# The low product of each 64-row score pair on all 128 rows

## The chip, the cores and the metric

The kernel runs on one core of a Trainium2 chip. The metric is the device time of one execution in microseconds (us); the median of the runs is compared. TensorE is called PE below (PEld is its weight load), VectorE DVE, ScalarE ACT, GpSimd POOL and SyncE SP, as the profile does.

## The reference

Two layers of a streaming encoder trunk over 512 tokens of width 2048, all in float32. Each layer normalises its input, multiplies it by one wide weight, and gives the columns to three attention mixers (MLA, DSA and differential attention), whose gated outputs go through an output projection; then a gated embedding is added. Cut to the scores that the change touches:

```python
# MLA: 128 plain features and 64 rotated ones; the rotated key is shared by the 6 heads
q = concat([q[..., :128], rope(q[..., 128:], pos, 64)]);  k = concat([k_nope, rope(k_rope, pos, 64)])
sc = einsum('bqhd,bkhd->bhqk', qb, k) * 192 ** -0.5
# DSA indexer: 8 heads of 64 rows, one key of 64 rows for all
rel = relu(einsum('bqhd,bkd->bqhk', qib, ki));  score = einsum('bqhk,bqh->bqk', rel, wb)
top_val, top_idx = lax.top_k(where(mask, score, NEG_INF), 128)     # the chosen keys of a query
# differential attention: 5 heads of two halves of 64 rows
a1 = softmax(mask(einsum('bqhd,bkhd->bhqk', qb[..., 0, :], k1) * 64 ** -0.5))
a2 = softmax(mask(einsum('bqhd,bkhd->bhqk', qb[..., 1, :], k2) * 64 ** -0.5))
o = einsum('bhqk,bkhd->bqhd', a1 - lam * a2, v)
```

## The kernel before

**Exact products from parts.** PE multiplies float32r values in one pass, which carries only part of float32. So each operand is split into a high part (an ACT copy that rounds) and a low part (what is left, a DVE subtraction), by `split_into`, and `mm3` (lines 369 to 371) forms a product of two split operands in three passes: high by high, high by low, low by high. Nearly all PE work is `mm3`: the input projection (`pp<-g,wh` in the profile), the output projection and the embedding gate, over 16 feature tiles of 128 rows.

**Pairs of 64 rows.** Where the summed dimension has 64 rows, `stack` lays a query's high part in one half of the 128 partitions and its low part in the other (`[hi; lo]` or `[lo; hi]`), and `twice` lays the key's high part in both halves. One pass over 128 rows then gives high by high and low by high. That is the first product of `mm2`, line 376. The second product, line 377, adds high by low: it takes the 64 rows of the query's tile that hold its high part, and the same 64 rows of a tile with the key's low part:

```python
a = TOP if half == 0 else LOW
PE.matmul(ps, q[:, qs], hi[:, :n], start=start, stop=False)      # line 376
PE.matmul(ps, q[a, qs], lo[a, :n], start=False, stop=stop)       # line 377
```

A pair has a width n of 128, 256, 384 or 512 keys, one for each block of 128 queries and the keys it may see. There are 88 pairs in a layer: 6 heads by 4 blocks in MLA, 8 heads by 3 blocks in the indexer (block 0 needs no choice), and 5 heads by 2 halves by 4 blocks in differential attention. So lines 376 and 377 stand in the profile with 176 instructions each.

**Low parts of the keys.** `twice` makes one low part by a DVE subtraction on 64 rows, 512 wide. Called without `lo`, as for the keys that MLA and the indexer share (`keys["r"]`, `keys["i"]`), it lays the low part in both halves, with two subtractions (lines 287 and 289). In differential attention `diff_ready` gives it a tile `kl` for both halves of a head: the low part of the first half goes to the upper 64 partitions, that of the second to the lower 64, one subtraction each (line 287).

**What sets the order.** The projection runs a chunk of weights at a time: SP loads a chunk (`wr`), ACT makes its high part (`wh`), DVE its low part (`wl`, line 363), and PE takes both. Two side streams are recorded between the chunks, each for a share of the projection's time: `mixers()` (MLA, then the indexer, then `heads()`), and `choose()`, which finds the 128 largest scores of each query by 16 rounds of `MAX` and `MATCH_REPLACE` on DVE (lines 786 and 787). `heads()` has the operands of the next head made (`diff_ready`) while the present one ends. A scheduler then orders each engine's instructions by a simulated timeline; on the chip each engine takes its own in that fixed order. All large temporaries are tiles `g` of one pool of 59 slots; scores go to PSUM tiles `at`, projections to `pp`.

Of the kernel before, what the change touches and what calls it, by code (L numbers as in the profile page):

```python
# [33 lines left out]
# columns of w_in  # L34
# [11 lines left out]
def rope_order():  # L46
    """Rows of 64: groups of 8, x1 then x2 of the frequencies 4i, 4i+2, 4i+1, 4i+3."""
    first, freq = [], []
    for r in (0, 2, 1, 3):
        for second in (0, 1):  # L50
            for i in range(8):
                freq.append(4 * i + r)
                first.append(1 - second)
    return np.array(freq), np.array(first)
# [65 lines left out]
class Stream:  # L120
    """Where each chunk [128, kt * cols] of one layer's weight lies in its flat array."""
# [19 lines left out]
def host_arrays(inputs):  # L141
    a = {k: np.asarray(v) for k, v in inputs.items()}

    def chunks(w, cols):
        """[K, n] at columns -> chunk after chunk of [128, 2, n]."""
        k = w.shape[0] // 128
        x = w[:, cols].reshape(k // 2, 2, 128, len(cols))
        return x.transpose(0, 2, 1, 3).reshape(-1)

    w_in = np.stack([np.concatenate([chunks(a["w_in"][i], c) for c in GROUP_COLS]) for i in range(DEPTH)])  # L150

    def square(w):
        return np.stack([np.concatenate([chunks(w[i], np.arange(512 * g, 512 * g + 512)) for g in range(4)])
                         for i in range(DEPTH)])

    order = np.concatenate([128 * m + np.arange(128) for m in MIX_ORDER])
    w_o = square(a["w_o"][:, order])
    w_pg = square(a["w_pg"])
    w_ple = square(a["w_ple"])

    uq, ukv = [], []
    for i in range(DEPTH):
        q, kv = [], []
        for j in range(3):
            h = (2 * j, 2 * j + 1)
            cols = np.concatenate([192 * x + np.arange(128) for x in h] + [192 * x + 128 + PERM_A for x in h])
            x = a["w_uq"][i][:, cols].reshape(3, 128, 384)
            q += [x[:2].transpose(1, 0, 2).reshape(-1), x[2].reshape(-1)]
            cols = np.concatenate([256 * h[0] + np.arange(128)] + [256 * x + 128 + np.arange(128) for x in h])
            kv += [chunks(a["w_ukv"][i], cols), chunks(a["w_ukv"][i], 256 * h[1] + np.arange(128))]  # L170
        uq.append(np.concatenate(q))
        ukv.append(np.concatenate(kv))

    def col(g):
        return g.reshape(-1, 128).T

    cc = np.concatenate([col(a["norm_g"]), col(a["q_norm_g"]), col(a["kv_norm_g"]), col(a["subln_g"]),
                         col(a["final_g"])], axis=1)
    lam = np.stack([a["lam_q1"], a["lam_k1"], a["lam_q2"], a["lam_k2"]], axis=1).reshape(1, DEPTH * 256)
    base = (500000.0 ** (np.arange(32) / 32.0)).astype(np.float32)  # L180
    inv = (np.float32(1.0) / base).astype(np.float32)
    rc = np.zeros((128, 8), np.float32)
    for half in range(2):
        s = slice(64 * half, 64 * half + 64)
        rc[s, 0] = inv[FREQ]
        rc[s, 1] = np.where(FIRST == 1, -1.0, 1.0)
    rc[:32, 2] = 1.0
    for half in range(2):
        rc[64 * half:64 * half + 16, 4] = 1.0
    rc[:, 3] = 1.0 - rc[:, 2]  # L190
    rc[:, 5] = 1.0 - rc[:, 4]
    c = np.ascontiguousarray
    return {
        "x": c(a["x"][0].T), "p": c(a["p"][:, 0].transpose(0, 2, 1)), "positions": c(a["positions"]),
        "w_in": w_in, "w_o": w_o, "w_pg": w_pg, "w_ple": w_ple,
        "w_uq": np.stack(uq), "w_ukv": np.stack(ukv), "cc": c(cc), "lam": c(lam), "rc": rc,
    }
# [3 lines left out]
def trunk(ctx: ExitStack, tc: tile.TileContext, t, out):  # L201
# [66 lines left out]
    def stack(y):  # L268
        """Of the two halves of 64 rows: [hi; lo] of the first, [lo; hi] of the second."""
        res = []  # L270
        for a, b in ((TOP, LOW), (LOW, TOP)):
            o = slot(F32R)
            ACT.activation(o[a], y[a], AF.Copy)
            DVE.tensor_tensor(o[b], y[a], f32(o[a]), op=ALU.subtract)
            res.append(o)
        return res

    def twice(y, half, lo=None):
        """hi of 64 rows in both halves, and lo, there or in both halves as well."""
        a, b = (TOP, LOW) if half == 0 else (LOW, TOP)  # L280
        hi = slot(F32R)
        ACT.activation(hi[a], y[a], AF.Copy)
        ACT.activation(hi[b], y[a], AF.Copy)
        both = lo is None
        if both:
            lo = slot(F32R)
        DVE.tensor_tensor(lo[a], y[a], f32(hi[a]), op=ALU.subtract)
        if both:
            DVE.tensor_tensor(lo[b], y[a], f32(hi[a]), op=ALU.subtract)
        return hi, lo  # L290
# [21 lines left out]
    def col_sums(parts):  # L312
        """sums over the partitions, a column [128 tokens, 1] for each block of the parts"""
# [7 lines left out]
    def rsqrt(dst, src, n, size):  # L321
        """1 / sqrt(mean + eps), from the table's root and a step of Newton's"""
# [12 lines left out]
    def spread(cols):  # L335
        """columns [128 tokens, 4] -> the same row of 512 on every partition, in PSUM."""
# [30 lines left out]
    def mm3(ps, l, r, start, stop):  # L367
        """ps += l^T r to float32's accuracy, of parts that one pass each carries."""
# [4 lines left out]
    def mm2(ps, q, qs, hi, lo, n, half, start, stop):  # L373
        """ps += of 64 rows: q stacked [hi; lo], hi in both halves, lo in this one."""
        a = TOP if half == 0 else LOW
        PE.matmul(ps, q[:, qs], hi[:, :n], start=start, stop=False)
        PE.matmul(ps, q[a, qs], lo[a, :n], start=False, stop=stop)
# [8 lines left out]
    streams, done = [], set()  # L386

    class Side:
        """Work that is emitted between the chunks of a projection, a share of their time."""
# [5 lines left out]
        def step(self):  # L395
            """False where it cannot go on before another chunk."""
# [26 lines left out]
    def products(ps, src, us, load, one):  # L423
        """ps of 16 feature tiles of the source: load(c) gives a chunk's 2 pairs, one(m, k, pair) multiplies."""
        nm = len(ps)
        for c in range(8):
# [6 lines left out]
            else:  # L433
                # A product at a time, so that the first are there early.
# [8 lines left out]
    def group_t(name, layer, stream, first, nm, src, gcol=None):  # L443
        """nm tiles of 128 features by 512 tokens; src: 16 pairs of [128, 512]."""
# [11 lines left out]
    def group_tok(name, layer, stream, first, n, src, gcol):  # L456
        """4 blocks of 128 tokens by n features"""
# [74 lines left out]
    def table(kind, R):  # L532
        """The tables of a branch, times the norm's factor of each token."""
# [8 lines left out]
    def rope(src, cs, rows=slice(0, 128), eng=POOL):  # L542
        """src * cos + swap(src) * sin -> float32 in a temporary."""
# [10 lines left out]
    def soft(ps, n, scale, e):  # L554
        """e = exp(scale * (ps - max)); returns 1 / sum."""
# [7 lines left out]
    def causal(ps, i):  # L563
        """the last 64 keys are hidden from the first 64 queries of block i"""
        DVE.memset(ps[0:64, 128 * i + 64:128 * i + 128], NEG)

    def attend(probs, v):
        """out^T [dv, tokens] in PSUM of probabilities [q, keys] per block; v(kb): pair [128 keys, 128]."""
# [22 lines left out]
    for L in range(DEPTH):  # L591
# [10 lines left out]
        def factors():  # L602
            """the norm's factor of each token, as columns and spread over the partitions"""
# [79 lines left out]
        def mla():  # L683
# [9 lines left out]
            for j in range(3):  # L693
# [30 lines left out]
                for x in range(2):  # L724
# [5 lines left out]
                    for i in range(NB):  # L730
# [4 lines left out]
                        mm2(ps[:, :n], q[2][x], qs, kr[0], kr[1], n, x, False, True)  # L735
# [15 lines left out]
        bias, score = {}, {}  # L751

        def indexer():
# [3 lines left out]
            for x in range(I_H):  # L757
# [4 lines left out]
                for i in range(1, NB):  # L762
# [3 lines left out]
                    mm2(ps[:, :n], q[x % 2], qs, ki[0], ki[1], n, x % 2, True, True)  # L766
# [35 lines left out]
        def diff_ready(x):  # L802
            q = stack(rope(raw.pop(("qc", x)), tab["c"]))
            y = rope(raw.pop(("kc", x)), tab["c"])
            kl = slot(F32R)
            return q, [twice(y, c, kl)[0] for c in range(2)], kl, value_parts("vc", x)

        def diff_probs(x, ops, probs):
            q, k, kl, _ = ops
            for i in range(NB):  # L810
# [5 lines left out]
                for c in range(2):  # L816
                    ps = at()
                    mm2(ps[:, :n], q[c], qs, k[c], kl, n, c, True, True)
# [50 lines left out]
        def heads():  # L869
            """the heads of both mixers; the operands of the next are made ahead"""  # L870
# [147 lines left out]
    def finals(s, R, pool_tiles):  # L1018
        """the tiles times the norm's factors, two at a time"""
# [71 lines left out]
```

## Time and profile before

| what | value |
|---|---|
| median of 3 runs | 2401.24 us (2401.13 to 2401.72) |
| the profiled execution: its span, first to last instruction | 2399.5 us |
| median less that span | 1.7 us |
| mean granted PE clock | 0.993 |
| busy ACT, POOL | 1067.6 us (44%), 486.1 us (20%) |
| DMA, mean over the span | 100 GB/s |

The page gives busy time, not useful time: a PE instruction's duration includes the time that it spends in the pipeline, so PE's rows overlap, and a PE that is shown busy may still start its products further apart than it could. How fast it goes is read from the distance between the starts of neighbouring instructions in the timeline.

### The profile page before, as it was taken

What the parts mean: (1) busy time and instruction counts of PE and PEld (TensorE: products, weight loads), DVE (VectorE), ACT (ScalarE), POOL (GpSimd) and SP (SyncE); (2) the same over time, 40 slices, a digit from 0 to 9 for tenths busy, and PEclk for the clock granted to TensorE, in tenths of its full rate; (3) what the DMA queues carried; (4) which work ended last, traced back from release to release, by engine and by line L of the source; (5) the groups of instructions that cost most, each with busy time, mean ns of one, the idle gap of its engine ahead of it and who ended that gap; (6) DMA issues with size and microseconds to landing.
All of it is one profiled execution on the core that took longest, in us unless ns stands there. A gap on an engine that the chain in (4) does not pass through costs nothing. (4 is left out here: it accounts for less than half of the span.)

```text
span 2399.5 us, 31043 instructions
## 1 busy us (share of the span) xinstructions
PE 2352.9 (98%) x11362; PEld 1956.7 (82%) x11372; DVE 1473.9 (61%) x2846; ACT 1067.6 (44%) x1989; POOL 486.1 (20%) x393
## 2 busy tenths in 40 slices
PE   8999999999999999999999999999999999999997
PEld 6899977777888788878888998777787887888887
DVE  8655557976667734344466555599667676543345
ACT  6444444454555423233345444444545554232444
POOL 4210122111232301011230110211122322220023
PEclk9999999999999999999999999999999999999998
DMA  5233322232233322322322333222222233232234
GB/s 182 73 95 94 121 78 81 84 101 88 97 97 110 112 98 98 105 88 97 97 88 77 92 112 102 81 84 97 82 99 93 97 111 113 97 106 97 97 105 159
DMA packets 88569, 239.03 MB, mean 100 GB/s; under 512 B 9440, under 2 KB 25312, under 8 KB 88416
## 3 DMA queue, kind: packets, MB, share of 16 engines
q1 hardware_dynamic: 84064, 223.41, 28.9%
q0 software_dynamic: 4352, 13.64, 1.5%
q8 instruction: 89, 1.46, 0.3%
q14 instruction: 64, 0.52, 0.1%
HBM read 219.19 MB, written 17.83 MB: 99 GB/s over the span
## 5 line engine op out<-in xcount | busy, mean ns | idle before, releaser
L369 PE MATMUL pp<-g,wh 128*128 128x512 f32 (+1 forms) x2432 | 942.4, 389 | 10.1 <-ACT g L263 6.0
L370 PE MATMUL pp<-g,wh 128*128 128x512 f32 (+1 forms) x2432 | 940.8, 387 | 0.0
L371 PE MATMUL pp<-g,wl 128*128 128x512 f32 (+1 forms) x2432 | 922.4, 388 | 15.3 <-DVE wl L363 15.2
L363 DVE SCALAR_TENSOR_TENSOR wl<-wr,cc,wh 128x512 fp32r<-128x512 f32 (+4 forms) x554 | 437.1, 799 | 327.3 <-ACT wh L362 316.8
L362 ACT ACTIVATE wh<-wr,cc 128x512 fp32r<-128x512 f32 (+4 forms) x554 | 361.8, 661 | 519.1 <-PE pp L370 339.4
L371 PEld LDWEIGHTS pp<-g,wl 128*128 128x128 f32 x2432 | 457.1, 189 | 109.5 <-DVE wl L363 18.5
L369 PEld LDWEIGHTS pp<-g,wh 128*128 128x128 f32 x2432 | 459.2, 189 | 105.7 <-ACT g L263 6.9
L370 PEld LDWEIGHTS pp<-g,wh 128*128 128x128 f32 x2432 | 458.7, 189 | 90.7 <-issue 2.2
L359 DVE TENSOR_TENSOR wl<-wr,wh 128x512 fp32r<-128x512 f32 x288 | 219.1, 771 | 356.1 <-ACT wh L358 332.0
L358 ACT ACTIVATE wh<-wr 128x512 fp32r<-128x512 f32 x288 | 177.9, 629 | 404.7 <-PE pp L370 370.0
L370 PE MATMUL pp<-wl,g 128*128 128x384 f32 (+2 forms) x512 | 158.5, 312 | 0.0
L371 PE MATMUL pp<-wh,g 128*128 128x384 f32 (+2 forms) x512 | 156.9, 310 | 0.0
L546 POOL TENSOR_TENSOR t<-z,cos 128x512 f32<-128x512 f32 (+1 forms) x50 | 71.4, 1429 | 393.6 <-DVE e L822 239.2
L369 PE MATMUL pp<-wh,g 128*128 128x384 f32 (+2 forms) x512 | 147.2, 319 | 0.0
L307 POOL TENSOR_TENSOR acc<-acc,t 128x512 f32<-128x512 f32 x41 | 59.1, 1441 | 298.6 <-ACT t L306 294.9
L264 DVE TENSOR_TENSOR g<-t,g 128x512 fp32r<-128x512 f32 x78 | 104.0, 1337 | 20.8 <-ACT g L263 20.8
L647 POOL DMA_DIRECT2D o_d<-t x32 | 18.2, 570 | 398.5 <-ACT t L645 398.5
L370 PEld LDWEIGHTS pp<-wl,g 128*128 128x128 f32 x512 | 96.6, 189 | 1.2 <-issue 0.4
L369 PEld LDWEIGHTS pp<-wh,g 128*128 128x128 f32 x512 | 93.0, 189 | 5.2 <-issue 2.7
L371 PEld LDWEIGHTS pp<-wh,g 128*128 128x128 f32 x512 | 96.4, 189 | 0.7 <-issue 0.5
L559 ACT ACTIVATE e<-at,sm 128x128 f32<-128x128 f32 (+3 forms) x128 | 66.7, 523 | 66.0 <-DVE sm L558 62.6
L547 POOL TENSOR_TENSOR t<-t,sin 128x512 f32<-128x512 f32 (+1 forms) x50 | 68.3, 1379 | 128.1 <-DVE t L545 127.5
(222 smaller groups left out, 2817.9 us busy)
## 6 DMA issues: line engine op xcount, KB each, us to landing
wr<-in_w_in_dram SPq DMA_DIRECT2D x175, 512.0 KB, 3.4
wr<-in_w_pg_dram SPq DMA_DIRECT2D x72, 512.0 KB, 3.2
wr<-in_w_o_dram SPq DMA_DIRECT2D x64, 512.0 KB, 3.2
wr<-in_w_in_dram SPq DMA_DIRECT2D x32, 384.0 KB, 3.1
wr<-in_w_in_dram SPq DMA_DIRECT2D x34, 256.0 KB, 2.7
o_d<-t POOLq DMA_DIRECT2D x32, 256.0 KB, 2.3
g<-o_d SPq DMA_DIRECT2D x32, 256.0 KB, 4.5
wr<-in_w_in_dram SPq DMA_DIRECT2D x16, 264.0 KB, 2.7
```

The source lines that it names most:

```text
L264: DVE.tensor_tensor(lo, src, f32(hi), op=ALU.subtract)
L307: POOL.tensor_tensor(acc, acc, s, op=ALU.add)
L358: ACT.activation(hi, r, AF.Copy)
L359: DVE.tensor_tensor(lo, r, f32(hi), op=ALU.subtract)
L362: ACT.activation(hi, r, AF.Copy, scale=g)
L363: DVE.scalar_tensor_tensor(lo, r, g, f32(hi), op0=ALU.mult, op1=ALU.subtract)
L369: PE.matmul(ps, l[0], r[0], start=start, stop=False)
L370: PE.matmul(ps, l[0], r[1], start=False, stop=False)
L371: PE.matmul(ps, l[1], r[0], start=False, stop=stop)
L546: eng.tensor_tensor(a[rows], src[rows], cs[0][rows], op=ALU.mult)
L547: POOL.tensor_tensor(b[rows], b[rows], cs[1][rows], op=ALU.mult)
L559: ACT.activation(e, ps[:, :n], AF.Exp, bias=st[:, 1:2], scale=scale, accum_out=st[:, 2:3])
```

## The change

The second product of a pair takes the whole stacked query tile, the same stationary operand as the first, and all 128 rows of a tile that has the key's low part in both halves. It so also adds low by low, which the 64-row form left out. For that, `twice` always lays the low part in both halves, and `diff_ready` makes a low tile for each half of a head in place of the shared `kl`: two more DVE subtractions (64x512) and one more slot for each head, 20 subtractions in all. MLA and the indexer had both halves already. The changed file also has its comments and docstrings taken out, so its line numbers are a few lower: lines 376 and 377 are 371 and 372 there, 363 is 359, lines 287 and 289 are 284 and 285, 786 and 787 are 781 and 782.

```diff
-    def twice(y, half, lo=None):
+    def twice(y, half):
         a, b = (TOP, LOW) if half == 0 else (LOW, TOP)
-        hi = slot(F32R)
+        hi, lo = slot(F32R), slot(F32R)
         ACT.activation(hi[a], y[a], AF.Copy)
         ACT.activation(hi[b], y[a], AF.Copy)
-        both = lo is None
-        if both:
-            lo = slot(F32R)
         DVE.tensor_tensor(lo[a], y[a], f32(hi[a]), op=ALU.subtract)
-        if both:
-            DVE.tensor_tensor(lo[b], y[a], f32(hi[a]), op=ALU.subtract)
+        DVE.tensor_tensor(lo[b], y[a], f32(hi[a]), op=ALU.subtract)
         return hi, lo
...
-    def mm2(ps, q, qs, hi, lo, n, half, start, stop):
-        a = TOP if half == 0 else LOW
-        PE.matmul(ps, q[:, qs], hi[:, :n], start=start, stop=False)
-        PE.matmul(ps, q[a, qs], lo[a, :n], start=False, stop=stop)
+    def mm2(ps, q, qs, k, n, start, stop):
+        PE.matmul(ps, q[:, qs], k[0][:, :n], start=start, stop=False)
+        PE.matmul(ps, q[:, qs], k[1][:, :n], start=False, stop=stop)
...
-                        mm2(ps[:, :n], q[2][x], qs, kr[0], kr[1], n, x, False, True)
+                        mm2(ps[:, :n], q[2][x], qs, kr, n, False, True)
...
-                    mm2(ps[:, :n], q[x % 2], qs, ki[0], ki[1], n, x % 2, True, True)
+                    mm2(ps[:, :n], q[x % 2], qs, ki, n, True, True)
...
         def diff_ready(x):
             q = stack(rope(raw.pop(("qc", x)), tab["c"]))
             y = rope(raw.pop(("kc", x)), tab["c"])
-            kl = slot(F32R)
-            return q, [twice(y, c, kl)[0] for c in range(2)], kl, value_parts("vc", x)
+            return q, [twice(y, c) for c in range(2)], None, value_parts("vc", x)
...
         def diff_probs(x, ops, probs):
-            q, k, kl, _ = ops
+            q, k = ops[:2]
...
-                    mm2(ps[:, :n], q[c], qs, k[c], kl, n, c, True, True)
+                    mm2(ps[:, :n], q[c], qs, k[c], n, True, True)
```

What this does to the order is seen at three places. The sizes are those of the outputs, so the 64 or 128 rows that a product sums over do not show. First PE, in a burst of four indexer pairs in layer 0, before:

```order
L376 MATMUL at<-g 128x256
L377 MATMUL at<-g 128x256
L376 MATMUL at<-g 128x384
L377 MATMUL at<-g 128x384
L376 MATMUL at<-g 128x512
L377 MATMUL at<-g 128x512
L376 MATMUL at<-g 128x256
L377 MATMUL at<-g 128x256
L371 MATMUL pp<-g,wl 128x512
```

The same place on PE after the change:

```order
L371 MATMUL at<-g 128x256
L372 MATMUL at<-g 128x256
L371 MATMUL at<-g 128x384
L372 MATMUL at<-g 128x384
L371 MATMUL at<-g 128x512
L372 MATMUL at<-g 128x512
L371 MATMUL at<-g 128x256
L372 MATMUL at<-g 128x256
L367 MATMUL pp<-g,wl 128x512
```

Nothing moved here. PE's order is the same row by row up to the first head of differential attention in layer 0; from there on pairs and weight products are interleaved differently at many places, a few rows apart. Second DVE, where `diff_ready` prepares a middle head of layer 0 (the two subtractions of `stack`, line 274, and those of `twice`), before:

```order
L274 TENSOR_TENSOR g<-t,g 64x512 x2
L363 SCALAR_TENSOR_TENSOR wl<-wr,cc,wh 128x512 x2
L287 TENSOR_TENSOR g<-t,g 64x512 x2
L264 TENSOR_TENSOR g<-v,g 128x512
L363 SCALAR_TENSOR_TENSOR wl<-wr,cc,wh 128x512
L565 MEMSET at 64x64
```

And DVE at that head after the change:

```order
L274 TENSOR_TENSOR g<-t,g 64x512 x2
L284 TENSOR_TENSOR g<-t,g 64x512
L285 TENSOR_TENSOR g<-t,g 64x512
L284 TENSOR_TENSOR g<-t,g 64x512
L285 TENSOR_TENSOR g<-t,g 64x512
L264 TENSOR_TENSOR g<-v,g 128x512
L359 SCALAR_TENSOR_TENSOR wl<-wr,cc,wh 128x512 x3
```

Four subtractions stand in a row where two stood, and the two weight splits that stood between lines 274 and 287 are elsewhere. Third DVE again, where the preparation of a head falls among the rounds of `choose()`, before:

```order
L274 TENSOR_TENSOR g<-t,g 64x512
L787 MATCH_REPLACE g<-top,g 128x512
L363 SCALAR_TENSOR_TENSOR wl<-wr,cc,wh 128x512 x2
L787 MATCH_REPLACE g<-top,g 128x256
L363 SCALAR_TENSOR_TENSOR wl<-wr,cc,wh 128x512
L786 MAX top<-g 128x8
L287 TENSOR_TENSOR g<-t,g 64x512
L786 MAX top<-g 128x8
L287 TENSOR_TENSOR g<-t,g 64x512
```

And after the change:

```order
L274 TENSOR_TENSOR g<-t,g 64x512
L359 SCALAR_TENSOR_TENSOR wl<-wr,cc,wh 128x512
L781 MAX top<-g 128x8
L782 MATCH_REPLACE g<-top,g 128x384
L782 MATCH_REPLACE g<-top,g 128x512
L359 SCALAR_TENSOR_TENSOR wl<-wr,cc,wh 128x512
L782 MATCH_REPLACE g<-top,g 128x256
L284 TENSOR_TENSOR g<-t,g 64x512
L285 TENSOR_TENSOR g<-t,g 64x512
L781 MAX top<-g 128x8 x2
L284 TENSOR_TENSOR g<-t,g 64x512
L285 TENSOR_TENSOR g<-t,g 64x512
```

Here too the two added subtractions stand beside the two old ones, and the weight splits (line 363, now 359) stand at other places among the rounds.

## The prediction

> **What bounds the kernel now.** I read the page's head first, then the list of PE's waits, then the groups by shape for the lines that change, and last PE's timeline around them, since only starts tell how fast PE goes.
>
> ```profile
> span 2399.5 us, 31043 instructions
> PE 2352.9 (98%) x11362; PEld 1956.7 (82%) x11372; DVE 1473.9 (61%) x2846; ACT 1067.6 (44%) x1989; POOL 486.1 (20%) x393
> PE pp L371 <- DVE wl L363: 15.2, 7, 4.1
> ```
>
> PE is busy for 98% of the span; the last row is the largest of its waits (us in total, times, longest). So a shorter PE program shortens the kernel nearly one to one, as long as DVE at 61% keeps up. The span is 1.7 us under the 2401.24 us median; I sum against the span and add the 1.7 us back.
>
> ```profile
> L377 PE MATMUL at<-g 64*128 64x512 f32 x48 | 23.8, 495 | 0.0
> L376 PE MATMUL at<-g 128*128 128x512 f32 x48 | 21.3, 443 | 0.0
> L371 PE MATMUL at<-g 128*128 128x512 f32 x22 | 8.7, 396 | 0.0
> ```
>
> All three multiply 512 columns into the same kind of PSUM tile. The last, a 128-row product among 128-row products, takes 396 ns, the 64-row product 495, and the 128-row product next to it 443. Half the rows takes longer, and the neighbour suffers too. These durations hold the pipeline's length, so the price is read from starts.
>
> ```profile
> 1478.93 0.33 PE L371 MATMUL pp<-wh,g 128*128 128x384 f32 x1
> 1479.11 0.33 PE L369 MATMUL pp<-wh,g 128*128 128x384 f32 x1
> 1480.89 0.28 PE L371 MATMUL at<-g 128*128 128x256 f32 x1
> 1481.01 0.28 PE L376 MATMUL at<-g 128*128 128x256 f32 x1
> 1483.20 0.40 PE L371 MATMUL at<-g 128*128 128x512 f32 x1
> 1483.43 0.40 PE L376 MATMUL at<-g 128*128 128x512 f32 x1
> 1483.76 0.50 PE L377 MATMUL at<-g 64*128 64x512 f32 x1
> 1484.19 0.51 PE L369 MATMUL pp<-g,wh 128*128 128x512 f32 x1
> 1484.53 0.40 PE L370 MATMUL pp<-g,wh 128*128 128x512 f32 x1
> 1484.77 0.40 PE L371 MATMUL pp<-g,wl 128*128 128x512 f32 x1
> ```
>
> Start to start, 128-row products step by 0.18 us at 384 columns (first two rows), 0.12 at 256 (next two) and 0.23 at 512 (1483.20 to 1483.43). Around the 64-row product the steps of 512 columns are 0.33 before it, 0.43 its own and 0.34 behind it, then 0.24. That is 0.10 + 0.20 + 0.11 + 0.01 = 0.42 us too much for one product, and none of these rows has a wait on it.
>
> **The change part by part.** *Line 377 on 128 rows.* A burst of pairs shows the price where the products alternate:
>
> ```profile
> 326.40 0.28 PE L376 MATMUL at<-g 128*128 128x256 f32 x1
> 326.61 0.38 PE L377 MATMUL at<-g 64*128 64x256 f32 x1
> 326.92 0.44 PE L376 MATMUL at<-g 128*128 128x384 f32 x1
> 327.29 0.44 PE L377 MATMUL at<-g 64*128 64x384 f32 x1
> 327.65 0.50 PE L376 MATMUL at<-g 128*128 128x512 f32 x1
> 328.09 0.50 PE L377 MATMUL at<-g 64*128 64x512 f32 x1
> 328.51 0.38 PE L376 MATMUL at<-g 128*128 128x256 f32 x1
> 328.83 0.38 PE L377 MATMUL at<-g 64*128 64x256 f32 x1
> 329.14 0.50 PE L371 MATMUL pp<-g,wl 128*128 128x512 f32 x1
> 329.47 0.40 PE L369 MATMUL pp<-g,wh 128*128 128x512 f32 x1
> ```
>
> From 326.40 to 329.47 nine products take 3.07 us. At the steps of 128-row products they would take 4 x 0.12 + 2 x 0.18 + 3 x 0.23 = 1.53. The four pairs lose 1.54 us, 0.385 each. So each excursion from 128 rows to 64 and back costs 0.385 to 0.42 us, whatever the width.
>
> ```profile
> 406.46 0.39 PE L370 MATMUL pp<-g,wh 128*128 128x512 f32 x1
> 406.78 0.49 PE L377 MATMUL at<-g 64*128 64x128 f32 x2
> 407.20 0.50 PE L371 MATMUL pp<-g,wl 128*128 128x512 f32 x1
> 407.64 0.49 PE L377 MATMUL at<-g 64*128 64x128 f32 x2
> 408.06 0.50 PE L369 MATMUL pp<-g,wh 128*128 128x512 f32 x1
> 408.39 0.40 PE L370 MATMUL pp<-g,wh 128*128 128x512 f32 x1
> ```
>
> Where two 64-row products (128 and 256 wide, merged here as x2) follow each other, they share one excursion: 1.93 us from 406.46 to 408.39, against 3 x 0.23 + 2 x (0.06 + 0.12) = 1.05 at normal steps, with 0.06 an estimate for 128 columns as half of the 256 step. That is 0.44 for each two. Of the 176 products of line 377, 20 stand in ten such twos; the first are those shown. So PE loses 156 x 0.385 + 10 x 0.44 = 60.1 + 4.4 = 64.5 us by the burst, and 156 x 0.42 + 4.4 = 69.9 by the lone product. I take 65, nearer the burst: a stretch of four averages the rounding of the starts. After the change every product has 128 rows, and line 371's own product at 396 ns shows that a 128-row product into such a tile steps normally. The instruction count on PE stays.
>
> The Trainium skill has the cause, on the page "TensorEngine Tiling (Array Packing)", section "Key Properties": changing the tiling mode, not just the tile, drains TensorE. This trace agrees: a drain is bought on both sides of each excursion, and the two 64-row products in a row share one. The same skill's page "TensorE: Matmul & The Clock Gate", section "Why this matters for your kernels", speaks against the change: one product of few rows takes the same time as one of 128 rows, and only concurrency gains. By it alone the sum would be 0; it is the first rival below.
>
> *Twenty more subtractions.*
>
> ```profile
> L287 DVE TENSOR_TENSOR g<-t,g 64x512 fp32r<-64x512 f32 x24 | 16.4, 682 | 1.2 <-ACT g L282 1.0
> 500.00:600.00 100.00, 100.00 (x454) 79.09 (x454) 66.44 (x158) 52.90 (x105) 19.02 (x15) 1.00 0.26 87
> 400.00:500.00 100.00, 95.03 (x410) 74.93 (x409) 96.51 (x249) 42.50 (x83) 10.61 (x9) 0.98 0.30 96
> 1600.00:1700.00 100.00, 96.47 (x423) 76.24 (x423) 91.47 (x232) 44.87 (x90) 11.89 (x10) 0.98 0.28 95
> ```
>
> They are 20 x 0.68 = 13.6 us of DVE. Three heads of a layer are prepared where DVE is busy like 66.44 of 100 us (third number of the stretch 500 to 600; PE and PEld stand before it) with PE at 100.00: 34 us in 100 are idle, and they hide two subtractions of 1.4 us. The cover is gone only where DVE is full: 96.51 and 91.47 us of the stretches that hold the 16 rounds of `choose()`. There, or at their edge, two heads are prepared in each layer, so I take 4 x 2 x 0.68 = 5.5 us as paid, between 0 and 13.6.
>
> *What PE gives back in the full DVE stretches.*
>
> ```profile
> 400.00:500.00 100.00, 4.70 (x14) 2.27 (x14) 0.98 0.30 96
> 1600.00:1700.00 100.00, 4.71 (x12) 2.05 (x12) 0.98 0.28 95
> 460.15 9.32 DVE L264 TENSOR_TENSOR g<-t,g 128x512 fp32r<-128x512 f32 x1
> 470.19 0.50 PE L371 MATMUL pp<-g,wl 128*128 128x512 f32 x1 [2.68 <-DVE wl L363]
> ```
>
> The same two stretches, counted for line 377 alone, hold 14 and 12 of its products. Where DVE ends last, what PE saves becomes a wait for `wl`: at most 26 x 0.385 = 10 us. PE was still busy for 95.03 and 96.47 us of them, so its buffers carry it most of the way; I take 4, with 0 and 10 as ends. One stall there has a cause of its own: a subtraction that took 9.32 us, where line 287 averages 0.68, and PE then lacked a weight for 2.68 us. Whether the new order meets such a subtraction again the order can't say; both signs, 0 taken, about 5 us either way (two layers by 2.7).
>
> *The extra slot* for each head: no row of PE's waits names a slot, so 0. *Accumulation and weights:* line 377 loads the same number of weights as before; 0.
>
> Sum: 2399.5 - 65 + 5.5 + 4 = 2344.0, and 1.7 for the rest of the execution: 2346 us.
>
> **The rivals.**
> - *Rows don't set the step.* If the loss came from short groups in `at` tiles or from changing the target tile, the 128-row form would keep it, and with the subtractions hidden or not the time would be 2401 to 2401 + 13.6 = 2415. For it: the rule above, and the fact that no row shows line 377 at 128 rows. Against it: lines 371 and 376 at 1483.20 and 1483.43 are in the same group and tile and step by 0.23. Chance 0.04.
> - *Half the gain.* If only the product's own step and not its neighbours' came from the rows, 166 excursions x 0.20 = 33 us go, against the 9.5 paid: 2401 - 33 + 9.5 = 2378. Against it: the neighbours at 1483.43 and 1484.19 are weight and score products that step normally elsewhere. Chance 0.05.
> - *DVE takes more of it.* All 10 us of the full stretches come back as waits, all 13.6 us of subtractions are paid, and PE waits 5 more: 2401 - 65 + 28.6 = 2365. Chance 0.11.
> - *Slower: the subtractions are caught.* If the two added ones of a head were each held like the one at 460.15, 9.32 us, the head would come 18.6 us later. That one cost PE 2.68, so 6.6 us of it were covered: 18.6 - 6.6 = 12 us a head, 120 in ten, 2346 + 120 = 2466. It decides where each head costs PE more than (2401 - 2346) / 10 = 5.5 us. Against it: the 24 subtractions of line 287 average 0.68 us, so hardly any was held. Chance 0.02.
> - *More gain.* The stalls at `wl` in the full stretches fall away and nothing is given back: 2401 - 70 - 5 = 2326 at the far end. Chance 0.06.
>
> **How the numbers follow.** The forecast of 2346 keeps the rest, 0.72. Its own terms span 2401 - 70 = 2331 to 2401 - 65 + 13.6 + 10 = 2360. I take 2330 to 2362 as the range: it leaves out half of the gain's far end (0.03), half of the case of DVE (0.05), the half gain (0.05), no gain (0.04) and slower (0.02), 0.19 in all. A change of 0.2% (5 us) is about what this kernel's measurement can tell from none. Faster: 0.72 + 0.05 + 0.11 + 0.06 = 0.94, and a fifth of the first rival, 0.01, makes 0.95; same takes half of that rival, 0.02; slower the rest and the fourth, 0.03.
>
> **What would show it.** In the profile after, line 372 (377 now) must have 128 rows and about 396 ns at 512 columns, line 371 the same in place of 443. In the burst of four indexer pairs, nine products must take about 1.53 us in place of 3.07. PE's instruction count must stay. The two stretches full of DVE must show more waiting for `wl` (over 5 us a layer means that the give-back is larger than I took), and the heads elsewhere none. The forecast is wrong if the steps around line 372 stay at 0.33 and 0.43, or if the rows for waits of PE on DVE grow from 15.2 us to 40 or more.

## The result and the profile after

The median went from 2401.41 us to 2330.22 us (four runs each, 2327.31 to 2332.91 after): a ratio of 0.9701, 95% interval 0.9689 to 0.9712, or 71.2 us less where 55 were forecast. The median lies at the low end of the range that was stated (2330 to 2362), and two of the four runs lie below it. The profiled execution's span went from 2399.5 to 2326.6 us.

The head of the page after, and the largest of PE's waits (us in total, times, longest):

```profile
span 2326.6 us, 31049 instructions
PE 2287.2 (98%) x11372; PEld 1950.5 (84%) x11372; DVE 1485.7 (64%) x2866; ACT 1065.6 (46%) x1989; POOL 495.0 (21%) x393
PE pp L367 <- DVE wl L359: 5.7, 3, 3.1
```

PE has its 98% again with 66 us less busy time. DVE has 20 instructions and 11.8 us more. PE's own count reads 11372 after 11362, but its weight loads count 11372 in both: ten of its records are missing in the profile before, and the change adds no product. The waits of PE on the weight's low part `wl` were forecast to grow from 15.2 us; they fell to 5.7.

The groups by shape of the two lines of a pair, 512 and 384 wide (instructions, busy us, mean ns):

```profile
L372 PE MATMUL at<-g 128*128 128x512 f32 x48 | 18.9, 394 | 0.0
L371 PE MATMUL at<-g 128*128 128x512 f32 x48 | 18.8, 392 | 0.0
L372 PE MATMUL at<-g 128*128 128x384 f32 x48 | 16.2, 337 | 0.0
```

The second product takes 394 ns where its 64-row form took 495, and its neighbour 392 in place of 443. The timeline of PE shows the same burst of four indexer pairs as before:

```profile
316.13 0.28 PE L371 MATMUL at<-g 128*128 128x256 f32 x1
316.24 0.28 PE L372 MATMUL at<-g 128*128 128x256 f32 x1
316.36 0.34 PE L371 MATMUL at<-g 128*128 128x384 f32 x1
316.54 0.34 PE L372 MATMUL at<-g 128*128 128x384 f32 x1
...
317.42 0.40 PE L367 MATMUL pp<-g,wl 128*128 128x512 f32 x1
317.65 0.39 PE L365 MATMUL pp<-g,wh 128*128 128x512 f32 x1
```

From 316.13 to 317.65 the nine products take 1.52 us in place of 3.07; 1.53 had been worked out from the steps of other 128-row products. So the price of an excursion was read rightly in this burst, and most of what was missed lies elsewhere. Of the 72.9 us that the span lost, the waits on `wl` alone are 9.5. These are stretches of 100 us around the rounds of `choose()` in layer 0 and 1 (PE, PEld, DVE, ACT, POOL busy, then the clock):

```profile
380.00:480.00 100.00, 100.00 (x464) 83.00 (x463) 99.06 (x270) 48.27 (x93) 12.93 (x10) 1.00 0.31 100
1540.00:1640.00 100.00, 100.00 (x467) 83.05 (x465) 95.04 (x254) 49.07 (x97) 16.45 (x13) 1.00 0.30 102
```

DVE is as full there as it was (99.06 of 100 us in layer 0), yet PE, which stood idle for 5.0 us of such a stretch before, now has no idle time. Before, DVE had been "busy" with one subtraction for 9.32 us; after, that subtraction (line 264, the low part that `diff_end` makes) is this row of DVE's timeline:

```profile
442.69 0.98 DVE L264 TENSOR_TENSOR g<-t,g 128x512 fp32r<-128x512 f32 x1
```

The experiments had to tell what each of the parts is worth alone: the rows of the product, the added subtractions, and the order that came with them.

### The profile page after: what moved, and what is told of

Read it like the earlier page. It is cut to its first block, busy times and chain, and to the rows that moved or that the text cites. A ratio compares the mean times of both kernels' runs of the same rounds, so it can differ in the third digit from the quotient of the medians.

```text
span 2326.6 us, 31049 instructions
## 1 busy us (share of the span) xinstructions
PE 2287.2 (98%) x11372; PEld 1950.5 (84%) x11372; DVE 1485.7 (64%) x2866; ACT 1065.6 (46%) x1989; POOL 495.0 (21%) x393
## 5 line engine op out<-in xcount | busy, mean ns | idle before, releaser
L359 DVE SCALAR_TENSOR_TENSOR wl<-wr,cc,wh 128x512 fp32r<-128x512 f32 (+4 forms) x554 | 447.5, 819 | 263.1 <-ACT wh L358 260.6
L264 DVE TENSOR_TENSOR g<-t,g 128x512 fp32r<-128x512 f32 x78 | 93.3, 1201 | 27.9 <-ACT g L263 27.9
L554 ACT ACTIVATE e<-at,sm 128x128 f32<-128x128 f32 (+3 forms) x128 | 67.1, 526 | 66.0 <-DVE sm L553 63.9
L979 POOL TENSOR_TENSOR t<-g 128x512 f32<-128x512 f32 x32 | 49.0, 1539 | 225.3 <-DVE g L264 207.1
```

The lines of the kernel that those rows point to most:

```text
L264: DVE.tensor_tensor(lo, src, f32(hi), op=ALU.subtract)
L359: DVE.scalar_tensor_tensor(lo, r, g, f32(hi), op0=ALU.mult, op1=ALU.subtract)
L554: ACT.activation(e, ps[:, :n], AF.Exp, bias=st[:, 1:2], scale=scale, accum_out=st[:, 2:3])
L979: POOL.tensor_tensor(r, f32(h[k][0]), f32(h[k][1]), op=ALU.add)
```

## The experiments

**The added subtractions alone** (edit of the kernel before):

```diff
-            kl = slot(F32R)
-            return q, [twice(y, c, kl)[0] for c in range(2)], kl, value_parts("vc", x)
+            kl = [twice(y, c) for c in range(2)]
+            return q, [w[0] for w in kl], [w[1] for w in kl], value_parts("vc", x)
...
-                    mm2(ps[:, :n], q[c], qs, k[c], kl, n, c, True, True)
+                    mm2(ps[:, :n], q[c], qs, k[c], kl[c], n, c, True, True)
```

> The added subtractions alone: each half of a differential head has a low tile of its own with the low part in both halves, but the second product still takes 64 rows. Theory A (the excursions to 64 rows cost about 65 us and the rest of the 71 us came from stalls of DVE that the new order avoids): 2392 to 2396, with no DVE subtraction of 9 us left in the stretch full of DVE. Theory B (the subtractions themselves cost their 5 to 14 us and the whole gain is PE's): 2406 to 2415. If the second product's rows do not matter at all and the order made the gain: 2330.

Measured: 2390.87 us against 2400.62, ratio 0.9964 (0.995 to 0.9978). More work on DVE, and 9.75 us less: a little more than theory A's 2392 to 2396, and theory B is out. PE's products are the 64-row ones still, so the gain has to come from the new order. PE's waits on `wl` fall from 15.2 us to 6.7, while 2.3 us of waits on a tile `z` are new (PE's waits, then DVE's and POOL's timelines):

```profile
PE pp L371 <- DVE wl L363: 6.7, 3, 4.1
PE pp L369 <- DVE z L910: 2.3, 2, 1.2
464.33 3.64 DVE L264 TENSOR_TENSOR g<-t,g 128x512 fp32r<-128x512 f32 x1
468.05 1.30 POOL L546 TENSOR_TENSOR t<-z,cos 128x512 f32<-128x512 f32 x1 [0.64 <-DVE g L264]
```

The subtraction takes 3.64 us here (3.61 in layer 1); it ends when POOL comes to an instruction that has to wait for DVE. PE has no idle time around it: 100.00 us busy of the 100 from 400 on, and from 1580 on in layer 1.

**The 128-row product alone.** Differential heads keep the shared low tile and two subtractions:

```diff
-        PE.matmul(ps, q[a, qs], lo[a, :n], start=False, stop=stop)
+        PE.matmul(ps, q[:, qs], lo[:, :n], start=False, stop=stop)
```

> The 128-row product alone: differential heads keep the one shared low tile and the two subtractions, and the second product takes all 128 rows of it, so it also adds the other half's low part times the query's low part. Theory A: 65 us less if the 9.3 us subtractions stay in DVE's stretch (2336), up to 72 less if the order moves them away (2329). Theory B (subtractions are paid): 2401 - 71 - 5 to 14, so 2316 to 2325.

Measured: 2331.23 us against 2400.62, ratio 0.9716 (0.9701 to 0.973). That is the time of the whole change to within its spread. The held subtraction is gone here as well (its row in this kernel's DVE timeline), so the new order did not need the added subtractions to lose it:

```profile
440.41 1.17 DVE L264 TENSOR_TENSOR g<-t,g 128x512 fp32r<-128x512 f32 x1
```

Beside the whole change this shows that the 20 subtractions, with the order that comes with them, cost nothing that these runs resolve: theory B's 2316 to 2325 is out, and the 5.5 us that the prediction paid for them are not there.

**128 rows in MLA and the indexer alone.** The order of every engine is that of the kernel before, row by row:

```diff
-    def mm2(ps, q, qs, hi, lo, n, half, start, stop):
+    def mm2(ps, q, qs, hi, lo, n, half, start, stop, rows=slice(0, 128)):
...
-        a = TOP if half == 0 else LOW
+        a = rows
...
-                    mm2(ps[:, :n], q[c], qs, k[c], kl, n, c, True, True)
+                    mm2(ps[:, :n], q[c], qs, k[c], kl, n, c, True, True, (TOP, LOW)[c])
```

> The 128-row product in MLA and the indexer alone (96 of 176 pairs); differential attention as before. All engines' orders are those of before, row by row. Excursion theory: 96 x 0.385 = 37 us less, 2364, and the held subtractions of 9.3 us stay. If only the product's own step is saved: 96 x 0.20 = 19 less, 2382. If the gain came from the new order: 2401.

Measured: 2362.62 us against 2400.62, ratio 0.9849 (0.9834 to 0.9864), 38.0 less where 37 was expected: 0.396 us for each of the 96 pairs. With no row moved, the held subtraction and the wait behind it stay as they were (DVE's timeline, PE's timeline, PE's waits):

```profile
441.75 9.31 DVE L264 TENSOR_TENSOR g<-t,g 128x512 fp32r<-128x512 f32 x1
451.78 0.79 PE L371 MATMUL pp<-g,wl 128*128 128x512 f32 x1 [2.67 <-DVE wl L363]
PE pp L371 <- DVE wl L363: 14.0, 8, 4.1
```

Of the 38.0 us, 1.2 are less waiting on `wl` (15.2 to 14.0). By the starts, the steps around 64-row products lose 26.8 us here in place of 63.9 before, so 37.1 for the 96 pairs, 0.386 each. This is the cleanest price of the excursion, and it settles the first two rivals of the prediction: the gain is neither nothing nor half (19). Nor is it a matter of order, since no order changed.

**Both products of a pair on 64 rows:**

```diff
-        PE.matmul(ps, q[:, qs], hi[:, :n], start=start, stop=False)
+        PE.matmul(ps, q[a, qs], hi[a, :n], start=start, stop=False)
```

> Both products of a pair on 64 rows of the same half (the first leaves out low by high), so 352 products of 64 rows in the same or fewer excursions. If the price is paid for each excursion from 128 rows to 64 and back: 2401 within 10 us, less where bursts of pairs now run through on 64 rows. If it is paid for each 64-row product: 176 x 0.2 to 0.385 more, 2436 to 2469.

Measured: 2369.44 us against 2400.62, ratio 0.9875 (0.986 to 0.989). Twice as many 64-row products, and 31 us less: the price is not one for each 64-row product. The orders of DVE, ACT and POOL differ here from the kernel before, so PE's steps say more than the time. PE's timeline shows a burst of four pairs (256, 384 and 512 wide, and one of another head, 256 wide; an x2 is two products of different width):

```profile
325.35 0.39 PE L370 MATMUL pp<-g,wh 128*128 128x512 f32 x1
325.67 0.38 PE L376 MATMUL at<-g 64*128 64x256 f32 x1
325.89 0.28 PE L377 MATMUL at<-g 64*128 64x256 f32 x1
326.01 0.39 PE L376 MATMUL at<-g 64*128 64x384 f32 x2
326.18 0.33 PE L377 MATMUL at<-g 64*128 64x384 f32 x2
326.35 0.39 PE L376 MATMUL at<-g 64*128 64x512 f32 x1
326.58 0.39 PE L377 MATMUL at<-g 64*128 64x512 f32 x1
326.91 0.50 PE L371 MATMUL pp<-g,wl 128*128 128x512 f32 x1
327.24 0.40 PE L369 MATMUL pp<-g,wh 128*128 128x512 f32 x1
```

Inside the burst 64-row products step like 128-row ones: 0.12 us from 325.89 to 326.01, 0.23 from 326.35 to 326.58. The loss sits at its two ends: 0.32 before 325.67 in place of 0.23, 0.22 behind it in place of 0.12, and 0.33 on each side of 326.91 in place of 0.23. These are 0.39 us for the eight products together.

The burst shows one thing more. From 326.01 on four products start before 326.35, two of 384 columns and two of 256. At the steps of 128-row products, 0.17 and 0.12, they would take 0.58 us; they take 0.34, because the 256-wide ones start within 0.06 us of the 384-wide ones. By the code (`x % 2`) neighbouring heads have their operands in opposite halves of the partitions. The trace doesn't record the half, but it shows that pairs of 64 rows ran side by side here. In the whole trace 68 products start early beside another one in this way, and win 9.1 us.

By the starts in the two traces, 352 products of 64 rows stand in 118 excursions here, against 176 in 166 before, and the steps at them lose 37.0 us against 63.9. Without the 9.1 us won side by side, and without a wait of 0.5 us that falls among them, the 118 excursions lose 45.6 us, 0.386 each; before it was 0.385. My 2401 "within 10 us" had counted neither how many excursions merge nor the products side by side.

Three more runs asked what held the subtraction. POOL's timeline in the kernel before, at the time of the 9.32 us, shows it without a gap from 460.17 to 468.9; the subtraction, begun at 460.15, ended at 469.47:

```profile
460.17 2.55 POOL L547 TENSOR_TENSOR t<-t,sin 128x512 f32<-128x512 f32 x2
462.67 1.30 POOL L920 TENSOR_TENSOR g<-g,z 128x512 f32<-128x512 f32 x1
...
467.66 1.25 POOL L548 TENSOR_TENSOR t<-t 128x512 f32<-128x512 f32 x1
```

**The held subtraction moved to POOL** (edit of the kernel before):

```diff
-            parts = split(s)
+            parts = slot(F32R), slot(F32R)
+            ACT.activation(parts[0], s, AF.Copy)
+            POOL.tensor_tensor(parts[1], s, f32(parts[0]), op=ALU.subtract)
```

> The kernel before with one thing moved: the subtraction of diff_end (the one that took 9.3 us on DVE in the stretch full of DVE) is done on POOL; 64-row products stay. If that held subtraction costs about 10 us in the two layers: 2389 to 2393, with waits of PE on wl in that stretch gone. If the order around it was the cost, or POOL becomes late: 2398 to 2405.

Measured: 2404.57 us against 2401.78, ratio 1.0011 (1.0002 to 1.0021): the first expectation failed. The trace says why. The next DVE instruction with two inputs in SBUF, a weight split, was held in its place (DVE's timeline), while POOL, with one instruction more in its row, ran without a gap from 459.73 to 469.68:

```profile
460.48 9.75 DVE L363 SCALAR_TENSOR_TENSOR wl<-wr,cc,wh 128x512 fp32r<-128x512 f32 x1 [0.69 <-ACT wh L362]
459.73 1.31 POOL L830 TENSOR_TENSOR g<-t,g 128x512 fp32r<-128x512 f32 x1
468.43 1.25 POOL L548 TENSOR_TENSOR t<-t 128x512 f32<-128x512 f32 x1
```

**The same edit on the changed kernel:**

> The changed kernel with the same subtraction moved to POOL. It has no subtraction over 2.3 us there and no wait of PE on wl in that stretch, so nothing is left to gain: 2326 to 2334. If DVE's load there still limits it: about 5 us less.

Measured: 2339.72 us, ratio 0.9744 to the kernel before (0.9729 to 0.9758), so 9.5 us slower than the changed kernel by the medians. Both expectations failed, since there was something to lose: the waits on `wl` are back, at a later head, where POOL's row is now longer by the subtraction (line 824) and runs from 581.70 to 589.17 without a gap. The weight split that PE waits for begins on DVE at 581.44 and is held for 8.28 us (PE's waits, then PE's, POOL's and DVE's timelines; the last POOL row begins behind a gap of 0.08 us, and DVE's row has the next split with it, x2):

```profile
PE pp L367 <- DVE wl L359: 12.2, 5, 4.1
589.77 0.50 PE L367 MATMUL pp<-g,wl 128*128 128x512 f32 x1 [2.78 <-DVE wl L359]
582.95 1.29 POOL L824 TENSOR_TENSOR g<-t,g 128x512 fp32r<-128x512 f32 x1
587.92 1.25 POOL L541 TENSOR_TENSOR t<-z,cos 128x512 f32<-128x512 f32 x1
589.25 1.62 POOL L543 TENSOR_TENSOR t<-t 128x512 f32<-128x512 f32 x1
581.44 9.98 DVE L359 SCALAR_TENSOR_TENSOR wl<-wr,cc,wh 128x512 fp32r<-128x512 f32 x2 [2.97 <-ACT wh L358]
```

**Two instructions taken out of POOL's row** (edit of the kernel before; DVE does these gates instead):

```diff
-                POOL.tensor_tensor(o, o, s, op=ALU.mult)
+                DVE.tensor_tensor(o, o, s, op=ALU.mult)
```

> The kernel before with the products of the MLA and DSA gates moved from POOL to DVE, so that POOL's row of instructions in the stretch full of DVE is two shorter. If the subtraction is held as long as POOL runs without a gap, it is held 2 x 1.3 us less (about 6.7 us) or not at all, and the time is 2392 to 2398. If holding has nothing to do with POOL: it still takes 9.3 us, and the 0.7 us more of DVE work for each gate leaves 2401 to 2404.

Measured: 2392.56 us against 2401.78, ratio 0.9961 (0.9948 to 0.9973). The subtraction is held for 5.61 us, a little less than expected, and it ends when POOL reaches its last instruction of the row (PE's waits, then DVE's and POOL's timelines):

```profile
PE pp L371 <- DVE wl L363: 10.2, 7, 4.1
461.09 5.61 DVE L264 TENSOR_TENSOR g<-t,g 128x512 fp32r<-128x512 f32 x1
461.12 2.54 POOL L547 TENSOR_TENSOR t<-t,sin 128x512 f32<-128x512 f32 x2
466.22 1.63 POOL L548 TENSOR_TENSOR t<-t 128x512 f32<-128x512 f32 x1
```

POOL has a small gap there, from 466.14 to 466.22, and DVE got in. DVE does more work in this kernel, in the stretch where it is full, and the time is 9 us less. The edit moves the gates of every MLA and DSA head, and other engines' rows with them, so not all of the 9 us is shown to be the hold's.

## Why the prediction was wrong

**Right: the excursion.** The step "line 377 on 128 rows" took 65 us. MLA and the indexer alone gave 38.0 us for 96 pairs, 0.396 each by the time and 0.386 by the steps, where 0.385 to 0.42 had been read. For all 176 pairs the steps in the kernel before lose 63.9 us, and from the run with the subtractions alone to the whole change the medians fall by 60.7. "Whatever the width" holds from 256 to 512 columns (0.39 to 0.40 for an excursion that stands alone); at 128 columns it is 0.34. The drain at each change of tiling mode, which the Trainium skill names in "TensorEngine Tiling (Array Packing)", section "Key Properties", agrees with the run with MLA and the indexer alone and with the one with 352 products, where the loss follows the count of excursions (0.386 us each) and not that of products. The rival by which rows don't set the step (2401 to 2415) fell, and so did the half gain (2378).

**Wrong, and the step that failed: "what PE gives back in the full DVE stretches".** It was put at +4 us, with the held subtraction entered at 0 and "about 5 us either way"; with the 5.5 us of the subtractions the order was to cost 9.5. The runs show -9.75 us in its place: with the subtractions alone, thus with 64-row products, the new order rids both layers of the 9.3 us subtraction. Two things were mis-sized. The give-back was taken from a DVE that was full of work, though about 9 of its 97 busy us were one held instruction, and without it DVE kept up with the faster PE. And the price of the hold was read from the 2.68 us wait behind it, twice, though more time was lost near it: a second wait of 2.29 us in the same stretch of layer 0, and PE's clock, which stood at half speed for 3.4 us in each layer, from 479.60, behind that second wait, and from 1653.80, at the end of layer 1's wait. The second wait's row, and three slices of the kernel before that hold these stretches, with their mean clock (the third number from the end):

```profile
478.27 1.21 PE L371 MATMUL pp<-g,wl 128*128 128x512 f32 x4 [2.29 <-DVE wl L363]
470.00:480.00 10.00, 7.52 (x32) 6.01 (x33) 9.88 (x25) 5.11 (x8) 0.00 (x0) 0.98 0.19 57
480.00:490.00 10.00, 10.00 (x39) 7.54 (x38) 9.92 (x28) 1.45 (x2) 0.00 (x0) 0.85 0.52 180
1650.00:1660.00 10.00, 7.32 (x26) 5.60 (x25) 9.93 (x17) 6.25 (x10) 2.85 (x3) 0.83 0.17 52
```

Of each 3.4 us at half speed up to 1.7 are lost: the 0.02, 0.15 and 0.17 that the slices lack, of 10 us each. The changed kernel has a clock of 1.00 in its full stretches. Whether all of this hangs on the hold is not shown: the run with MLA and the indexer alone keeps the hold, and its waits on `wl` in that stretch are 3.6 us in place of 5.0. Nor are the 9.75 us, a difference of medians, traced to the last: in the profiled execution with the subtractions alone the span is 8.0 us shorter (2391.5), with 8.5 us less waiting on `wl`, the 2.3 us on `z` that are new, and another stretch of 3.4 us at half speed, at 1997.20.

**Wrong: "twenty more subtractions".** 5.5 us were paid; the 128-row product without them (2331.23) and with them (2330.22) take the same time within their spread. The two differ in order too, so that each subtraction was hidden is not shown; that they cost nothing on balance is.

Put together, by the medians: the order and the subtractions, put at +9.5, gave -9.75, so the forecast was 19 us too high there; the excursions, put at -65, gave -60.7 in the new order, so it was 4 us too low there. These are 15 of the 16 us by which the forecast of 2346 missed. The rival "more gain", which held the same mechanism at its far end, had been given a chance of 0.06.

**What is shown of the hold, and what not.** The held instructions each read two tiles in SBUF, and they end 0.55 to 0.56 us after POOL's row ends or comes to a gap: at 469.47 after 468.91 before, at 467.97 after 467.42 with the subtractions alone, at 470.23 after 469.68 and 589.72 after 589.17 with the subtraction on POOL, at 466.70 after 466.14 with the gates on DVE. So the hold lasted as long as POOL's row in these five. Most holds cost PE little: the kernel before has ten DVE instructions of over 2.5 us (3.36 to 9.32), the changed one still eight (3.05 to 5.44), and PE's longest wait on `wl` behind those eight is 1.30 us.

Why the changed kernel escapes is only seen, not tested. Its POOL too runs with hardly a gap there, but the subtraction took 0.98 us, at another moment relative to POOL's instructions, and the two engines then slow each other in place of one waiting for the whole row (DVE's and POOL's timelines; such a weight split takes 0.73 us at 438.18, such a POOL instruction 1.29 at 444.78):

```profile
444.98 1.64 DVE L359 SCALAR_TENSOR_TENSOR wl<-wr,cc,wh 128x512 fp32r<-128x512 f32 x1
446.02 1.76 POOL L541 TENSOR_TENSOR t<-z,cos 128x512 f32<-128x512 f32 x1
```

No run here fixes that moment, so the order that escapes can't be foreseen from these traces.

## What to carry to other kernels

A matmul on 64 rows among matmuls on 128 rows is dear at both of its ends, 0.39 us for each excursion here, so fill the rows, with a redundant term if need be, or put the 64-row products next to each other. Here filling the rows was the faster of the two (2331 against 2369 us). Read PE's rate from the distance between starts: 98% busy hid 64 us. Before calling an engine full, look for single instructions that last many times their kind's mean; time that one held instruction takes can go away, or come back, with any change of the order, so such a stretch deserves a range with both signs as wide as all that hangs on it.

## What the runs showed of the hardware

Unexpected was how long a hold can be: a DVE subtraction of about 0.7 us took 9.32 us, 5.61 us and 3.64 us, and weight splits of 0.73 us took 9.75 and 8.28, each time until about 0.55 us after POOL's row of instructions had ended or paused. And 64-row products of one half, in a row, step as 128-row products do (0.12 us at 256 columns, 0.23 at 512), so fewer rows in one half gain nothing and lose nothing as long as the mode stays. Products of two pairs also ran side by side, in the burst shown by the code pairs of opposite halves: 68 early starts won 9.1 us.
